# Rolling a matrix in DRAM: row pieces dealt to the DMA engines in blocks of 32 rows instead of 64

## The chip, the cores and the metric

The kernel runs on one core of a Trainium2 chip. The metric is the device time of one execution in microseconds, lower being better.

## The reference

`x` is a matrix of 8192 by 8192 float32 numbers, and `shift` is 100. Each row is rotated to the right by 100 places:

```python
def reference(x, shift):
    return np.roll(x, shift, axis=1)
```

So `out[r, 100:] = x[r, :8092]` and `out[r, :100] = x[r, 8092:]`. There is no arithmetic. 268 MB are read and 268 MB are written; a row is 32 KB.

## The kernel before

The output's columns are divided at `a = 128`, the first multiple of 128 columns (512 bytes) at or above the shift; `g = a - s` is 28.

**Columns 128 and up** are the bulk: 8064 columns of each row, 32,256 bytes, copied straight from the input tensor to the output tensor in DRAM, with no stop on the chip. One `dma_start` (line 41) copies 16 row pieces. The rows are grouped by `xm` and `om`, views of the input and the output with the axes `c` (block), `j`, `e` and the columns. The axis `e` has 16 entries, and within one DMA it is the outer one, so that each of the core's 16 DMA engines copies one row piece. Which rows those are is set by `j`: entry `e` of a DMA is row `4e + j` of a block of 64 rows, so neighbouring engines are four rows apart. The four DMAs of a block take turns between two queues, `engines[j % 2]`: SP (the sync engine) has `j` 0 and 2, ACT (the scalar engine) has 1 and 3. In the last four blocks, 256 rows, every DMA is divided at column `mid` into two, so that the last pieces are shorter. In all SP and ACT issue 248 whole and 16 half DMAs each. The framework gives each queue four semaphores in turn: an issue waits until the DMA four places earlier on its queue has landed, so up to eight DMAs are under way.

**Columns 0 to 127** go through the chip, on GpSimd's queue and VectorE, beside the bulk. Rows are taken in 16 groups of 512, four rows to a partition (`Q = 4`). For each group, GpSimd loads a tile `t` (line 70: the end of a row together with the start of the next, which lie next to each other in memory), and two small pieces of a tile `h` (lines 71 and 74); VectorE copies the rest of `h` from `t` (lines 72 and 75). After all loads are issued, GpSimd stores the 16 tiles `h` to the output (line 78). These tiles all have their own buffers. Nothing in the bulk waits for this part, nor the other way round.

The branch `if a > 512` isn't taken with this shift.

Of the kernel before, what the change touches and what calls it, by code (L numbers as in the profile page):

```python
# [1 line left out]

# [4 lines left out]


@with_exitstack
def kernel(  # L10
    ctx: ExitStack,
    tc: tile.TileContext,
    x: bass.AP,
    shift: int,
    out: bass.AP,
):
    nc = tc.nc
    n_rows, n_cols = x.shape
    s = shift % n_cols
    a = -(-s // 128) * 128  # L20
    g = a - s
    P = nc.NUM_PARTITIONS
    engines = [nc.sync, nc.scalar]
    n_chunks = 16
    rows = n_rows // n_chunks

    xm = x.rearrange("(c e j) w -> c j e w", e=16, j=4)
    om = out.rearrange("(c e j) w -> c j e w", e=16, j=4)
    if a < n_cols:
        blocks = n_rows // 64
        mid = (a + n_cols) // 256 * 128
        for c in range(blocks):
            parts = ((a, mid), (mid, n_cols)) if c >= blocks - 4 and a < mid else ((a, n_cols),)
            for j in range(4):
                for lo, hi in parts:  # L40
                    engines[j % 2].dma_start(out=om[c, j, :, lo:hi], in_=xm[c, j, :, lo - s:hi - s])
    if a == 0:
        return


    if a > 512:
        for i in range(n_chunks):
            r = slice(i * rows, (i + 1) * rows)
            nc.gpsimd.dma_start(out=out[r, :s], in_=x[r, n_cols - s:])
            if g > 0:  # L50
                nc.gpsimd.dma_start(out=out[r, s:a], in_=x[r, :g])
        return

    Q = 4
    n_st = n_rows // (P * Q)
    reads = ctx.enter_context(tc.tile_pool(name="reads", bufs=n_st))  # L60
    heads = ctx.enter_context(tc.tile_pool(name="heads", bufs=n_st))
    xt = x.rearrange("(k p q) c -> k p q c", q=Q, p=P)
    ot = out.rearrange("(k p q) c -> k p q c", q=Q, p=P)
    tiles = []
    for k in range(n_st):
        t = reads.tile([P, Q - 1, a], x.dtype)
        h = heads.tile([P, Q, a], x.dtype)
        lead = bass.AP(tensor=x.tensor, offset=(k * P * Q + 1) * n_cols - s,
                       ap=[[Q * n_cols, P], [n_cols, Q - 1], [1, a]])
        nc.gpsimd.dma_start(out=t[:], in_=lead, single_packet=True)  # L70
        nc.gpsimd.dma_start(out=h[:, Q - 1, :s], in_=xt[k, :, Q - 1, n_cols - s:], single_packet=True)  # L71
        nc.vector.tensor_copy(h[:, :Q - 1, :s], t[:, :, :s])  # L72
        if g > 0:
            nc.gpsimd.dma_start(out=h[:, 0, s:], in_=xt[k, :, 0, :g], single_packet=True)  # L74
            nc.vector.tensor_copy(h[:, 1:, s:], t[:, :, s:])  # L75
        tiles.append(h)
    for k, h in enumerate(tiles):
        nc.gpsimd.dma_start(out=ot[k, :, :, :a], in_=h[:], single_packet=True)  # L78


# [1 line left out]
_INS = ['x', 'shift']  # L82
_OUTS = [((8192, 8192), 'float32')]

_NUMBERS = {'shift': 100}


# [26 lines left out]
```

## Time and profile before

| | before |
|---|---|
| median of 3 runs | 829.13 us (828.62 to 831.27) |
| profiled execution, first to last instruction | 818.3 us |
| median over the span | 10.8 us |
| payload moved, and mean rate | 272.71 MB, 333 GB/s |
| memory traffic, read and written | 656 GB/s over the span |
| VectorE busy, GpSimd busy | 7.8 us, 41.1 us |
| packets of SP's queue, ACT's queue, GpSimd's queue | 8448, 8448, 3328 |

The profiled execution's own time isn't listed apart from its span; the runs' median is 10.8 us longer than the span, and that is what lies ahead of the first and behind the last instruction.

How to read the views. The page gives the span in 40 equal slices of 20.5 us; a digit of the row "DMA" is the mean busy share of the 16 DMA engines in tenths (9 is 90% or more), and "GB/s" is the payload that they moved. A byte copied from DRAM to DRAM counts once in the payload and twice in the memory's traffic. Queue q1 and q10 are the hardware queues on which SP and ACT issue, q0 is GpSimd's. In the rows of DMA issues the last figure is the median time in microseconds from issue to landing. In the view of stretches the last three columns are the TensorE clock (of no account here), the DMA engines' busy share and the GB/s moved. In the view of waits the figures are microseconds in all, times, and the longest.

### The profile page before, as it was taken

Reading aid. Unit: us, or ns where it says so; the run is one execution under the profiler, and the core shown is the slowest. Engines: PE = TensorE matmul, PEld = TensorE weight load, DVE = VectorE, ACT = ScalarE, POOL = GpSimd, SP = SyncE. Lnnn points to the kernel's source line nnn. Section 1 sums busy time; section 2 is a strip of 40 time slices with the busy share of each in tenths; the row PEclk is TensorE's granted clock in tenths of the full one; section 3 lists DMA queues with packets and bytes.
Section 4 is the critical chain, followed back from the end, with each engine's and each line's share of the span. In section 5 each row is a group of like instructions: output and inputs, shape, how many; then the busy total and the mean of one; then the engine's idle time right before and its main releaser. Section 6 shows DMA issues by size and latency. Waiting matters only on the chain. (4 is left out here: it accounts for less than half of the span.)

```text
span 818.3 us, 689 instructions
## 1 busy us (share of the span) xinstructions
DVE 7.8 (1%) x32; POOL 41.1 (5%) x68
## 2 busy tenths in 40 slices
DVE  0000000000000000000000000000000000000000
POOL 3011111111010000000000000000000000000000
DMA  9999999999999999999999999999999999999998
GB/s 304 340 344 338 341 334 345 341 346 350 353 352 357 347 332 321 335 328 326 333 330 323 330 331 330 331 326 333 330 328 334 333 330 339 328 333 334 328 318 294
DMA packets 20229, 272.71 MB, mean 333 GB/s; under 512 B 9472, under 2 KB 9728, under 8 KB 11776
## 3 DMA queue, kind: packets, MB, share of 16 engines
q1 hardware_dynamic: 8448, 132.14, 48.2%
q10 hardware_dynamic: 8448, 132.14, 46.1%
q0 software_dynamic: 3328, 8.39, 4.7%
q14 instruction: 5, 0.04, 0.0%
HBM read 268.44 MB, written 268.44 MB: 656 GB/s over the span
## 5 line engine op out<-in xcount | busy, mean ns | idle before, releaser
L78 POOL DMA_DIRECT2D out_dram<-h x16 | 11.4, 712 | 87.2 <-DMA out_dram<-h 51.7
L70 POOL DMA_DIRECT2D t<-in_x_dram x16 | 12.1, 759 | 32.1 <-DMA h<-in_x_dram 31.3
L74 POOL DMA_DIRECT2D h<-in_x_dram x16 | 8.6, 538 | 85.7 <-DMA t<-in_x_dram 85.7
L71 POOL DMA_DIRECT2D h<-in_x_dram x16 | 8.9, 558 | 23.9 <-DMA h<-in_x_dram 23.9
L72 DVE COPY h<-t 128x300 f32<-128x300 f32 x16 | 5.9, 368 | 190.4 <-DMA t<-in_x_dram 190.4
L75 DVE COPY h<-t 128x84 f32<-128x84 f32 x16 | 3.2, 201 | 0.0
L95 POOL MEMSET const-float32-0.0<- 128x1 f32 x1 | 0.1, 99 | 0.2 <-issue 0.2
L95 POOL MEMSET const-bfloat16-1.0<- 128x1 bf16 x1 | 0.1, 101 | 0.0
L95 POOL MEMSET const-uint8-127<- 128x1 uint8 x1 | 0.1, 99 | 0.0
L95 POOL MEMSET const-float32-1.0<- 128x1 f32 x1 | 0.1, 98 | 0.0
## 6 DMA issues: line engine op xcount, KB each, us to landing
out_dram<-in_x_dram ACTq DMA_DIRECT2D x248, 504.0 KB, 12.5
out_dram<-in_x_dram SPq DMA_DIRECT2D x248, 504.0 KB, 12.5
out_dram<-h POOLq DMA_DIRECT2D x16, 256.0 KB, 63.0
t<-in_x_dram POOLq DMA_DIRECT2D x16, 192.0 KB, 32.6
out_dram<-in_x_dram SPq DMA_DIRECT2D x8, 256.0 KB, 5.9
out_dram<-in_x_dram ACTq DMA_DIRECT2D x8, 256.0 KB, 5.8
out_dram<-in_x_dram SPq DMA_DIRECT2D x8, 248.0 KB, 6.1
out_dram<-in_x_dram ACTq DMA_DIRECT2D x8, 248.0 KB, 6.1
```

Of the source, the lines that this page charges most:

```text
L70: nc.gpsimd.dma_start(out=t[:], in_=lead, single_packet=True)
L71: nc.gpsimd.dma_start(out=h[:, Q - 1, :s], in_=xt[k, :, Q - 1, n_cols - s:], single_packet=True)
L72: nc.vector.tensor_copy(h[:, :Q - 1, :s], t[:, :, :s])
L74: nc.gpsimd.dma_start(out=h[:, 0, s:], in_=xt[k, :, 0, :g], single_packet=True)
L75: nc.vector.tensor_copy(h[:, 1:, s:], t[:, :, s:])
L78: nc.gpsimd.dma_start(out=ot[k, :, :, :a], in_=h[:], single_packet=True)
L95: nc = _bacc.Bacc("TRN2", target_bir_lowering=False, num_devices=1)
```

## The change

The views group rows by `j=2` instead of `j=4`: a block has 32 rows and not 64, entry `e` of a DMA is row `2e + j`, and neighbouring engines are two rows apart instead of four. A block has two DMAs, one for SP (`j` 0) and one for ACT (`j` 1). There are 256 blocks instead of 128, and the last eight, again 256 rows, are halved. The number, sizes, queues and order of the DMAs are those of before; which rows a DMA holds, and so which addresses are under way at one time, differs. The rest of the diff is blank lines, which moves line 41 to 36 and line 109 to 99.

```diff
-    xm = x.rearrange("(c e j) w -> c j e w", e=16, j=4)
-    om = out.rearrange("(c e j) w -> c j e w", e=16, j=4)
+    xm = x.rearrange("(c e j) w -> c j e w", e=16, j=2)
+    om = out.rearrange("(c e j) w -> c j e w", e=16, j=2)
     if a < n_cols:
-        blocks = n_rows // 64
+        blocks = n_rows // 32
         mid = (a + n_cols) // 256 * 128
         for c in range(blocks):
-            parts = ((a, mid), (mid, n_cols)) if c >= blocks - 4 and a < mid else ((a, n_cols),)
-            for j in range(4):
+            parts = ((a, mid), (mid, n_cols)) if c >= blocks - 8 and a < mid else ((a, n_cols),)
+            for j in range(2):
                 for lo, hi in parts:
-                    engines[j % 2].dma_start(out=om[c, j, :, lo:hi], in_=xm[c, j, :, lo - s:hi - s])
+                    engines[j].dma_start(out=om[c, j, :, lo:hi], in_=xm[c, j, :, lo - s:hi - s])
```

## The prediction

> **What bounds the kernel now.** I read the page first (busy shares, the 40 slices, the DMA queues), then the waits of the SP queue, then the stretches side by side, then the DMA view of two stretches with different work in them, and last the writers of the output tensor. From the page:
>
> ```profile
> span 818.3 us, 689 instructions
> DVE 7.8 (1%) x32; POOL 41.1 (5%) x68
> DMA  9999999999999999999999999999999999999998
> GB/s 304 340 344 338 341 334 345 341 346 350 353 352 357 347 332 321 335 328 326 333 330 323 330 331 330 331 326 333 330 328 334 333 330 339 328 333 334 328 318 294
> q1 hardware_dynamic: 8448, 132.14, 48.2%
> q10 hardware_dynamic: 8448, 132.14, 46.1%
> q0 software_dynamic: 3328, 8.39, 4.7%
> HBM read 268.44 MB, written 268.44 MB: 656 GB/s over the span
> out_dram<-in_x_dram ACTq DMA_DIRECT2D x248, 504.0 KB, 12.5
> out_dram<-in_x_dram SPq DMA_DIRECT2D x248, 504.0 KB, 12.5
> ```
>
> No compute engine matters: VectorE and GpSimd are busy 1% and 5% of the span, while the 16 DMA engines are busy from the first slice to the last. The two hardware queues, SP's and ACT's, carry 264.3 of the 272.7 MB; these are the row pieces that go straight from the input to the output. The software queue (the first 128 columns) is 8.4 MB. The page's chain of waits is of no use for the end: it closes with GpSimd's last step at about 270 us, after which the row pieces run on alone for two thirds of the span.
>
> Does issuing hold the row pieces up? The waits of SP's queue, and the row of that line in the view of the output tensor:
>
> ```profile
> SPq L41 <- DMA out_dram<-in_x_dram: 671.1, 260, 4.8
> L41 SPq DMA_DIRECT2D out_dram<-in_x_dram x264: 509/510/842, 0.7 to 811.3; - x132
> DMA to landing us min/median/max: 4.1/12.5/16.8
> ```
>
> SP issues 264 DMAs at 510 ns each, 135 us, and stands 671 us in 260 waits for an earlier row DMA to land. All but its first four issues wait, so each queue keeps four DMAs under way, the two together eight, of 16 rows each: 128 rows. Eight times 516 kB in 12.5 us is 330 GB/s, which is the rate of the slices: the pieces land as fast as something behind the queue takes them, and issue is not it.
>
> Whether that something is the DMA engines or the memory is told by two stretches with different work:
>
> ```profile
> 200.00:250.00 50.00, 0.00 (x0) 4.97 (x7) 1.00 1.00 351
> 300.00:400.00 100.00, 0.00 (x0) 0.00 (x0) 1.00 1.00 328
> 600.00:700.00 100.00, 0.00 (x0) 0.00 (x0) 1.00 0.99 332
> 800.00:819.00 19.00, 0.00 (x0) 0.00 (x0) 1.00 0.84 281
> ```
>
> The last two columns are the DMA engines' busy share and the GB/s moved. The engines are full in the first three, yet they move 351 GB/s between 200 and 250 us, where GpSimd's stores run, and about 330 later. The DMA views of 0 to 270 us (first pair) and of 300 to 780 us (second pair) say why:
>
> ```profile
> DMA packets 8355, 92.42 MB, mean 342 GB/s; under 512 B 3575, under 2 KB 3831, under 8 KB 5729
> q0 software_dynamic: 3133, 7.78, 13.8%
> ...
> GB/s 333 319 332 328 333 336 325 331 331 328 325 323 339 312 333 325 328 339 323 333 333 320 336 339 331 331 333 323 337 337 331 331 336 336 328 336 331 325 336 328
> DMA packets 9847, 158.54 MB, mean 330 GB/s; under 512 B 4917, under 2 KB 4917, under 8 KB 4933
> ```
>
> A row piece touches the memory twice (read and write), a byte of the software queue once (its other side is on chip). Early: 2 x (92.42 - 7.78) + 7.78 = 177.1 MB in 270 us, 656 GB/s. Late: 2 x 158.54 = 317.1 MB in 480 us, 661 GB/s. Counted at the memory the two agree within 1%, though the payload differs by 4% and one stretch is full of pieces under 512 B. So the memory side sets the rate, at about 660 GB/s, and time is bytes divided by that.
>
> The Trainium skill, page "HBM Reference", section "Specifications (TRN2)", puts a stack that two cores share at about 716 GB/s. By that figure 536.9 MB could not take less than an estimated 750 us, so the kernel would stand at 92% of the limit; no run here shows 716.
>
> **The change, part by part.** *Count of work: nothing.* Before, 128 blocks of four DMAs, the last four blocks halved into two column parts; after, 256 blocks of two DMAs, the last eight halved. Either way a queue issues 248 whole DMAs and then 16 half ones, in the same sequence of sizes and with the same wait on the DMA four places earlier, and the halved part is the last 256 rows. GpSimd's and VectorE's lists are the same. So issue (135 us, hidden in 671 us of waiting), the depth of eight DMAs and the tail cost the same; if the tail's 281 GB/s moved by one per cent, it would be 0.2 us. GpSimd's 128 columns are not touched and end some 480 us before the row pieces do; were that cover gone, their 8.39 MB would cost about 25 us at 333 GB/s, but no part of the change takes it away.
>
> *What moves: the addresses at one time.* A row is 32 KB. Before, engine e of the 16 copies rows 4e to 4e+3 of a block of 64, alternating between the queues, then jumps 2 MB ahead: neighbours are 128 KB apart, 16 engines in step cover 2 MB, and each engine returns to the same 128 KB modulo 2 MB whatever it lags. After, engine e copies rows 2e and 2e+1 and jumps 1 MB: neighbours are 64 KB apart, engines in step cover 1 MB, and the fixed slot is 64 KB modulo 1 MB. The engines do lag: a queue's DMA takes 2 x 516 kB / 330 GB/s = 3.1 us on the average, but waits reach 4.8 us and landings range from 4.1 to 16.8 us. An engine that falls two packets behind its neighbour is always a whole block, 1 MB, behind after the change; before, half of the time it is still within the same block. Reads and writes do this alike, since input and output rows have the same place in their tensors.
>
> No row of this trace has a second spacing in it, so the cost is bounded from both sides by how far the rate varies under the present one, where the engines' lags change by themselves. The 23 slices of the page from 307 to 777 us, where row pieces run alone, average 330.2. The four slowest (321, 323, 326, 326) average 324, 1.9% less; the four fastest (339, 335, 334, 334) average 335.5, 1.6% more. Some of this is where a slice cuts a packet, so these are bounds and not readings. The finer slices of 300 to 780 us go down to 312, 5.8% more time per byte, and up to 339, 2.7% less. On about 780 us of full-rate copying, slow ends are +15 us and +45 us, fast ends -12 us and -21 us.
>
> I take half of the first slow end, +0.95% of 780 us: 7.4 us. It is nearest to the middle because nothing but the spacing changes; and to the slow side because the present rate sits on a level that two quite different mixes reach alike, as something does that is close to its limit. From there closer rows can lose much, and spread-out ones had little left to lose.
>
> At one place a rule speaks of spacing itself. The Trainium skill, page "DMA: Bandwidth & Descriptors", section "Latency and other measured facts", has copies between HBM tensors losing rate at large power-of-two row pitches: 207 GB/s per direction at 512 KiB, 164 at 2 MiB, 103 at 4 MiB, with the cause inferred only. Both spacings here lie below its smallest; by it the change is worth nothing (829 us), or something if its fall begins earlier than it was looked for. This trace has 330 GB/s per direction at 128 KB, above all of its figures.
>
> **The sum.** Span 818.3 + 7.4 = 825.7 us. The median of the runs, 829.13, is 10.8 us over the profiled span; this lies outside the first and last instruction and stays. Forecast: 829.1 + 7.4 = 836.5 us. About 0.3% (2.5 us) is what a measurement of this kernel can tell from no change: its three runs lie that far apart.
>
> **The rivals.**
>
> *No difference.* The memory's level is a limit of bytes and not of where they lie; the two mixes at 656 and 661 GB/s speak for it, as do the lags, which scatter the rows before and after. Against it: slices of one mix still differ by 5%. Time: 829 us.
>
> *Faster.* The present 128 KB between neighbours makes some engines collide: sixteen rows that agree in all address bits below 128 KB ask the same part of the memory when they run in step. At 64 KB one more bit differs among the sixteen, so half as many agree in all of them. The place is the whole of the row copying; it decides if collisions that need 128 KB alignment cost more than what is lost by crowding into 1 MB. For it: the payload is well under the fastest slices' rate at times, with the engines' share at 0.99 to 1.00, so engines do stand waiting inside packets. Against it: the flat 660. Price: the fast end, 1.6% of 780 us, -12 us, 817 us; at most -21 us, 808 us.
>
> *Much slower.* The crowding holds engines in step, so that the worst mutual position lasts, not passes. Then the rate is that of the slowest fine slice, 312: +45 us, 874 us; halfway to it, 852 us. For it: with two rows per visit in place of four, every engine jumps twice as often, at the same moment when in step. Against it: landings from 4.1 to 16.8 us show engines not in step.
>
> *That the change does not do what it says* is no rival: the first dimension of each DMA is still 16 rows, one to an engine, and only the stride between them differs.
>
> **How the numbers follow.** Slower by a little (832 to 845 us) 0.45; much slower 0.12; no difference 0.17; faster 0.26. The likeliest is the first, so the time is 836.5 us; its own range is 832 to 845 us. To leave out no more than 2 in 10 the range reaches past the fast end of 817 to 815 us and past halfway to the worst slice, to 857 us: what is left out is the extreme of the fast case and the upper half of the much slower one. Faster 0.26, same 0.17, slower 0.45 + 0.12 = 0.57.
>
> **What would show it.** If right: the profile after has the same counts of packets and DMAs, the engines' share stays at 0.99 to 1.00, the slices from 307 to 777 us average about 327 in place of 330.2, the stretch of 0 to 270 us falls in the same proportion, and the median time to landing goes from 12.5 to about 12.6 us. The tail stays at some 280 GB/s. No difference shows as 330 again; faster as 335 with landings near 12.3 us. The step that can fail is the sign: nothing in this trace fixes it, and a mean over 333 between 300 and 780 us makes the forecast wrong. A change in one stage only, or in SP's 510 ns, would say that it is not the spacing at all.

## The result and the profile after

Over 22 runs each, the changed kernel takes 827.17 us (median; 825.03 to 830.82) and the kernel before 829.68 us (826.53 to 831.27). The ratio is 0.9973, 95% interval 0.9963 to 0.9984. So the change is a gain of 0.27%, clear of noise, and just inside the 0.3% that the prediction had called "same". The forecast, 836.5 us, had the sign wrong. The range, 815 to 857 us, holds the time, but only because it was stretched to the end of the rival "faster"; the range of the forecast's own case, 832 to 845 us, doesn't. Here and below a ratio compares the runs within 1.5% of a kernel's fastest with those of before taken beside them, while a single time is the median of all its runs.

These rows of the page after answer to those shown of before:

```profile
span 823.6 us, 689 instructions
DMA  9999999999999999999999999999999999999998
GB/s 300 345 338 345 325 338 340 332 344 359 341 341 345 338 337 323 332 332 321 329 331 331 324 329 331 332 326 329 332 326 329 336 323 337 320 335 337 321 312 302
q1 hardware_dynamic: 8448, 132.14, 47.8%
q10 hardware_dynamic: 8448, 132.14, 46.7%
HBM read 268.44 MB, written 268.44 MB: 652 GB/s over the span
out_dram<-in_x_dram ACTq DMA_DIRECT2D x248, 504.0 KB, 12.6
out_dram<-in_x_dram SPq DMA_DIRECT2D x248, 504.0 KB, 12.6
```

The waits of SP's queue, the row of its line among the writers of the output, two stretches, and the DMA view of 300 to 780 us:

```profile
SPq L36 <- DMA out_dram<-in_x_dram: 678.2, 260, 4.6
L36 SPq DMA_DIRECT2D out_dram<-in_x_dram x264: 509/510/756, 0.7 to 818.1; - x132
300.00:400.00 100.00, 0.00 (x0) 0.00 (x0) 1.00 1.00 328
600.00:700.00 100.00, 0.00 (x0) 0.00 (x0) 1.00 1.00 331
...
DMA packets 9824, 157.97 MB, mean 329 GB/s; under 512 B 4904, under 2 KB 4904, under 8 KB 4929
```

Packets, queues, issue time (510 ns) and the number of waits (260) are those of before. The engines are full. Between 300 and 780 us 157.97 MB were moved where it was 158.54 MB: 0.36% less, though the runs are 0.27% faster. The prediction's own sign for this stretch (327 GB/s if slower, 330 if the same, 335 if faster) reads 329, no difference. That is the first lesson: one profiled execution of each kernel can't show a difference of this size, and these two point the wrong way.

The span of after is 823.6 us in an execution that took 825.38 us, so 1.8 us lie outside the span. In every execution of which both are on record, 68 of before among them, it is 1.7 to 1.8 us. So the profiled execution of before, with its span of 818.3 us, took about 820 us, less than any timed run of that kernel (the fastest took 826.53 us). The 10.8 us that the prediction and the part ahead of it took for time outside the span are for the most part the distance of one quick execution from the median; why it was quick isn't known. From here on the timed ratios decide, and profiles are read only for differences of several per cent.

### The profile page after: what moved, and what is told of

Its sections match the earlier page's. It is cut to its first block, busy times and chain, and to the rows that moved or that the text cites. A ratio compares the mean times of both kernels' runs of the same rounds, so it can differ in the third digit from the quotient of the medians.

```text
span 823.6 us, 689 instructions
## 1 busy us (share of the span) xinstructions
DVE 7.8 (1%) x32; POOL 41.1 (5%) x68
## 3 DMA queue, kind: packets, MB, share of 16 engines
q0 software_dynamic: 3328, 8.39, 4.7%
```

## The experiments

Except where said, only the deal of the bulk's rows differs. The loop is written as a list of DMAs, so that `J` can be any number and the last 16 DMAs, again 256 row pieces, are the halved ones; `J = 2` and `J = 4` give after and before:

```diff
-            for j in range(2):
+        deals = [(c, j) for c in range(n_rows // (16 * J)) for j in range(J)]
+        for n, (c, j) in enumerate(deals):
...
-                    engines[j].dma_start(...)
+                    engines[n % 2].dma_start(...)
```

**Other powers of two: 1, 8, 64 and 512 rows.** `J = 1`:

> Neighbouring engines one row (32 KB) apart, blocks of 16 rows; all else as in the kernel after. Theory A (the memory's level counts bytes, not places): no move, 829 us or within 0.3% of before. Theory B (crowding costs, the forecast's): since two rows apart did not cost, one row apart shows the cost later: slower by 1% or more, 838 us up. Theory C (alignment at 128 KB costs, closer is better): a further step of the same sign and size as that from four rows to two, 824 to 826 us.

`J = 8`:

> Neighbouring engines eight rows (256 KB) apart, blocks of 128 rows. Theory A: 829 us, within 0.3% of before. Theory B: a little faster than before, 824 to 829 us. Theory C: slower than before by the step from two rows to four or more, 832 us up.

`J = 64`:

> Neighbouring engines 64 rows (2 MB) apart, eight blocks of 1024 rows. Theory A: 829 us. Theory B: 829 us or less. Theory C: clearly slower, because sixteen engines agree in six more address bits than at 32 KB; by the Trainium skill, page DMA: Bandwidth & Descriptors, the rate at a row pitch of 2 MiB is 164 in place of 207, which would be an estimated 829 x 207 / 164 = 1046 us.

`J = 512`:

> Each engine copies its own 512 rows one after the other, neighbours 16 MB apart. Theory A: 829 us. Theory B: 829 us or less. Theory C: much slower than at 2 MB, over 1000 us.

Measured: one row 833.42 us, ratio 1.0056 (1.0030 to 1.0082); eight rows 831.16 us, 1.0024 (1.0011 to 1.0037); 64 rows 1366.87 us (six runs, 1281.79 to 1444.80), 1.5478 (1.5436 to 1.5519); 512 rows 2110.99 us (six runs, 1981.24 to 2258.35). The fastest of the last is 2.39 times the median of before beside it (829.39 us). No theory got all four. Theory A holds at eight rows and fails at one, and at 64 rows by far: places matter, and greatly. Theory B, the forecast's, has the direction right at one row, though not its 1%, and is refuted by 64 and 512 rows: wide spacing is not safe. Theory C has the direction right at 8, 64 and 512 rows (at eight the time stays just under its 832 us) and fails at one row. The page of the kernel with 64 rows, its SP waits, and the same view of waits for 512 rows:

```profile
span 1372.4 us, 689 instructions
DMA  9999999999999999999999999999999999999999
GB/s 214 246 256 226 245 228 227 213 211 221 201 195 191 194 193 191 187 190 189 204 189 185 187 183 203 182 181 183 183 194 189 185 182 182 197 189 191 183 189 168
out_dram<-in_x_dram SPq DMA_DIRECT2D x248, 504.0 KB, 21.8
SPq L36 <- DMA out_dram<-in_x_dram: 1220.9, 260, 9.1
...
SPq L36 <- DMA out_dram<-in_x_dram: 1901.7, 260, 14.9
```

This is the execution of 1374.21 us, 199 GB/s in the mean. The busy digits are the same nines as at 333 GB/s. In the trace's packet records a whole row piece, one packet of 32,256 bytes, takes 1.19 us at the least in both kernels, but 2.57 us in the median with 64 rows and 1.42 us in before. An engine counts as busy for all of that time, so the share tells nothing of a loss of 40%; GB/s and the time to landing (21.8 us in place of 12.5) do. By the Trainium skill, page "DMA: Bandwidth & Descriptors", section "Latency and other measured facts", copies lose rate at power-of-two pitches above 512 KiB. The direction agrees; the estimate from its figures, 1046 us at 2 MiB, is well under the fastest run of 64 rows, 1281.79 us.

**Is it distance or agreement of addresses? 60 rows.** Blocks of 960 rows, then the last 512 rows four apart:

```diff
+    J, J2, split = 60, 4, 7680
+    for lo_r, hi_r, jj in ((0, split, J), (split, n_rows, J2)):
```

> Neighbouring engines 60 rows (1.875 MB) apart in eight blocks of 960 rows, the last 512 rows as in before. The distance is nearly that of 64 rows, but 60 rows is an odd multiple of 128 KB, as the four rows of before are. If distance itself costs (pages of memory far apart): near the 1367 us of 64 rows, over 1250 us. If agreement in the address bits below 2 MB costs: back at the level of before, 822 to 840 us.

Measured: 844.07 us, 1.0190 (1.0167 to 1.0213). Of the 55% that 64 rows cost, 1.9% is left at nearly the same distance, a little above the 840 us of the second reading. So most of the loss is not how far apart the engines are; it goes with a spacing that is a large power of two. In its stretches the rate is steady and a little low:

```profile
400.00:500.00 100.00, 0.00 (x0) 0.00 (x0) 1.00 1.00 321
500.00:600.00 100.00, 0.00 (x0) 0.00 (x0) 1.00 1.00 321
600.00:700.00 100.00, 0.00 (x0) 0.00 (x0) 1.00 1.00 323
```

**Is it closeness or an odd spacing that costs at one row? Three rows**, `J, J2, split = 3, 2, 8160`:

> Neighbouring engines three rows (96 KB) apart in blocks of 48 rows, the last 32 rows dealt two apart. If crowding within a block is what made one row 0.56% slower than before, three rows lies between two (0.9973) and four: 826 to 830 us. If it is the odd row (each queue's rows no longer all of one parity, neighbours that differ in the lowest row bit), it lies near one row: 832 to 835 us.

Measured: 834.00 us, 1.0053 (1.0037 to 1.0069). It is like one row, in a block wider than the 32 rows of after, so the width of the block alone is not what orders these times. That it is oddness was this experiment's other reading. Six and 12 rows below show that even spacings can lose more, so oddness isn't needed for a loss; whether it is what one and three rows lose by isn't shown.

**Is it the bulk itself? The bulk alone, four and two rows apart**, without GpSimd's part:

```diff
-    if a == 0:
-        return
+    return
```

> The bulk alone, four rows apart as in before; columns 0 to 127 of the output are left out. If memory traffic at some 660 GB/s is the bound in all stages, 8.39 MB of software traffic in 660 GB/s is 12.7 us less than before: about 816 us. If the small pieces cost more than their bytes, lower, down to 800 us.

> The bulk alone, two rows apart as in after; columns 0 to 127 are left out. If the 0.27% of the change lies in the bulk copying by itself: 2 us under bulk4. If it lies in how the bulk meets GpSimd's small pieces: equal to bulk4 within 1 us.

Measured: 814.64 us (0.9822, 0.9802 to 0.9841) with four rows and 811.92 us (0.9792, 0.9775 to 0.9809) with two. The difference is 2.7 us, the whole effect of the change and of the same sign, though the two intervals overlap a little. So it can lie in the bulk alone and needs no meeting with the small pieces. Leaving those out saves 14.8 us (1.78% of 829): a little more than the 12.7 us of their bytes at 660 GB/s. Their packets held 4.7% of the engines' time in before, 38 us of the span; that so much less was saved says that bytes at the memory set their price, and not the engines' time. Rows of the page of the kernel with four:

```profile
GB/s 305 329 329 317 329 331 318 332 323 320 329 332 336 312 337 326 331 331 328 332 326 329 336 317 326 334 325 329 328 331 327 330 328 326 329 325 328 328 316 290
HBM read 264.24 MB, written 264.24 MB: 652 GB/s over the span
```

Without the small pieces the early slices fall to the level of the late ones. The 334 to 357 GB/s of before's first stage (its second to thirteenth slice) came with the software queue's bytes, which touch the memory once, as the prediction had counted.

**Six rows**, 192 KB, `J, J2, split = 6, 4, 8064`:

> Neighbouring engines six rows (192 KB, an odd multiple of 64 KB) apart in blocks of 96 rows, the last 128 rows four apart. If agreement in address bits sets the small differences too, it equals two rows apart, 0.997 of before: 826 to 828 us. If the width of the block does, it lies between four rows and eight: 829 to 831 us. If anything but a power of two costs, as three rows and 60 may be read: 832 us up.

Measured: 843.47 us, 1.0168 (1.0136 to 1.0199). It is the third outcome: slower than four and eight rows, though it lies between them, and though its spacing agrees in the same low address bits as two rows.

**Two rows apart, the queues on neighbouring blocks:**

```diff
+        deals = [(c + d, j) for c in range(0, blocks, 2) for j in range(2) for d in range(2)]
```

> Two rows apart as in after, but the two queues copy the same j of two neighbouring blocks, so the two packets that an engine has in hand are 1 MB apart and not adjacent rows. If the adjacency of an engine's two rows is what two and four rows have and one row lacks: 0.5% slower than after, 831 to 834 us. If only the spacing of the engines counts: as after, 826 to 828 us.

Measured: 828.43 us, 0.9990 (0.9974 to 1.0006). This lies between after (0.9973) and before and can't be told from before; it is far from 0.5% slower than after. So the lack of adjacent rows in an engine's hand is not what makes one row slow. But neither is it shown that spacing alone gives the gain of after: with the spacing kept and the order changed, no gain clear of noise is left.

**16 rows**, `J = 16`:

> Neighbouring engines 16 rows (512 KB) apart, blocks of 256 rows. Between 8 rows (1.0024) and 64 rows (1.55). If the loss begins where the Trainium skill, page DMA: Bandwidth & Descriptors, sees it, past a pitch of 512 KiB: 831 to 836 us. If it grows with every bit in which the engines agree: 850 us up.

Measured: 886.52 us (four runs, 873.97 to 890.56), 1.0601 (1.0531 to 1.0672). The large loss begins above eight rows, a spacing of 256 KB. The Trainium skill, page "DMA: Bandwidth & Descriptors", same section as above, has 207 GB/s per direction at 512 KiB of row pitch, against 214 that it calls full; for engines 512 KB apart the measurement says 6% slower. Rows of the stretches, from the execution of 890.56 us:

```profile
400.00:500.00 100.00, 0.00 (x0) 0.00 (x0) 1.00 1.00 301
600.00:700.00 100.00, 0.00 (x0) 0.00 (x0) 1.00 0.99 296
700.00:800.00 100.00, 0.00 (x0) 0.00 (x0) 1.00 0.99 296
```

**Writes alone.** The input isn't read; the bulk is written from a tile on the chip, and columns 0 to 127 are left out:

```diff
-                engines[n % 2].dma_start(out=om[c, j, :, lo:hi], in_=xm[c, j, :, lo - s:hi - s])
+                engines[n % 2].dma_start(out=om[c, j, :, lo:hi], in_=w[n % 8::8, lo - s:hi - s])
```

> The bulk alone, four rows apart, written from a tile on the chip: reading the input is left out, and columns 0 to 127 too. If the memory's traffic of reads and writes together is the bound, the same writes run at well over 330 GB/s, up to whatever the DMA engines take: under 700 us. By the Trainium skill, page DMA: Bandwidth & Descriptors, section Specifications, 435 GB/s is that ceiling, an estimated 608 us for 264 MB. If the engines, the eight DMAs under way or the issue were the bound: about 815 us, as bulk4.

One run: 698.78 us, just under 700. The stretches show more than the total:

```profile
0.00:100.00 100.00, 6.88 (x1) 0.20 (x4) 1.00 0.90 235
100.00:200.00 100.00, 0.00 (x0) 0.00 (x0) 1.00 1.00 368
200.00:300.00 100.00, 0.00 (x0) 0.00 (x0) 1.00 1.00 424
300.00:400.00 100.00, 0.00 (x0) 0.00 (x0) 1.00 1.01 428
400.00:500.00 100.00, 0.00 (x0) 0.00 (x0) 1.00 1.01 428
500.00:600.00 100.00, 0.00 (x0) 0.00 (x0) 1.00 1.01 421
```

The same 16 engines, with the same eight DMAs under way, hold 421 to 428 GB/s once the source is on the chip. Reads alone were not run, so it might be asked whether the engines are slower where the source is in DRAM. The packet records answer it: a whole row piece takes 1.19 us at the least in this kernel and in before alike, and 16 engines at that pace would move an estimated 433 GB/s. The median is 1.19 us here and 1.42 us in the copy, where about a quarter of the pieces go at the quick pace. So an engine can copy from DRAM to DRAM as fast as it writes, and what holds the copy at 330 is the waiting inside the packets: the memory side. Why the first 200 us ran at 235 and 368 GB/s is open; nothing moves for the first 9.4 us, in which the tile is filled.

**Spacing or length of visit?** The change does two things: neighbours come closer, and an engine copies two rows in a block and not four. Here the spacing of before is kept with visits of two rows:

```diff
+        deals = [(c + d, h + j) for c in range(0, blocks, 2) for h in (0, 2) for d in range(2) for j in range(2)]
```

> Neighbours four rows apart as in before, but an engine copies two rows of one block, two of the next, then the other two of each: visits of two rows as in after. If the 0.27% of the change comes from the spacing: as before, 828 to 830 us. If it comes from the shorter visit: as after, 826 to 828 us.

Measured: 831.58 us, 1.0026 (1.0012 to 1.0039), slower than both readings. At four rows the short visit brings no gain; in this order it costs. So shorter visits by themselves don't explain the gain of after.

**12 rows**, `J, J2, split = 12, 4, 8064`, and **32 rows**, `J = 32`:

> Neighbours 12 rows (384 KB) apart in blocks of 192 rows, the last 128 rows four apart. If places that wander are what costs (a block that is no power of two of rows, so that engines with different lags come to one another's places): as six and 60 rows, 841 to 846 us. If the loss at six rows came from that one distance, or agreement in bits below 128 KB counts (12 is an odd multiple of four): 828 to 833 us.

> Neighbours 32 rows (1 MB) apart, blocks of 512 rows. If the loss grows with the number of engines that share a place in a fixed stretch of memory (none at 8 rows, 1.06 at 16, 1.55 at 64): between, about 1.2 to 1.4 of before, 990 to 1160 us. If 64 rows has a cause of its own: about 1.06 to 1.12, under 930 us.

Measured: 12 rows 840.08 us, 1.0125 (1.0104 to 1.0145), close to six and 60 rows, just under the 841 us of the first reading and far from the second; 32 rows 1068.00 us, 1.2830 (1.2777 to 1.2882), between 16 and 64 as the first reading said. The slices of 32 rows:

```profile
span 1073.1 us, 689 instructions
GB/s 251 282 257 274 285 260 288 278 269 271 271 293 281 265 260 263 274 259 257 257 255 262 247 244 249 226 254 228 243 221 250 210 250 207 253 225 245 230 236 236
```

**All spacings together**, as ratios to before:

| rows between neighbours | ratio |
|---|---|
| 1, 2, 4, 8 | 1.0056, 0.9973, 1, 1.0024 |
| 3, 6, 12, 60 | 1.0053, 1.0168, 1.0125, 1.0190 |
| 16, 32, 64, 512 | 1.060, 1.283, 1.548, 2.39 |

One picture fits these three rows; it is inferred, since no view shows memory addresses. Suppose that two packets hinder each other when their rows have nearly the same place within a fixed stretch of memory, some 4 MB (128 rows). With 1, 2, 4 or 8 rows each of the 16 engines keeps to places of its own, whatever it lags, since blocks divide the stretch. With 16 rows two engines share a place, with 32 four, with 64 eight, with 512 all of them, and the loss grows in that order. With 3, 6, 12 and 60 rows the blocks don't divide the stretch, engines that lag wander over one another's places, and a small loss comes up, in no order of spacing. The picture has no place for the 0.56% of one row, and only the runs of 12 and 32 rows put it to the test.

## Why the prediction was right and wrong

**The bound: right.** The memory side sets the time, at about 660 GB/s of reads and writes with spacings in the flat part of the table. Writes alone showed that the engines can move 421 to 428 GB/s, and the bulk alone that 8.39 MB less of traffic is worth 14.8 us, where the count at the memory gives 12.7. But 660 GB/s is no fixed limit of bytes: 64 rows move the same bytes at 391 GB/s over the span of their profile.

**No cost in count, issue, depth and tail: right.** The rows after are the same, 264 issues of 510 ns and 260 waits among them; the tail's last slices are 312 and 302 GB/s where they were 318 and 294.

**What moves: the description was right, the conclusion drawn from it was not.** The prediction said that each engine returns to the same 128 KB modulo 2 MB whatever it lags, and to 64 KB modulo 1 MB after. It went on to count a narrower place as crowding: "closer rows can lose much, and spread-out ones had little left to lose". This is the step that failed, in both halves. Going from four rows to two gained 0.27%, though three rows and one lost 0.53% and 0.56%; the spread-out powers of two lost 0.24% at eight rows and 6% to 139% at 16 to 512. By the picture above, which is inferred, places that are half as wide are still places of one engine alone, and the large losses come where engines share a place, which going from four rows to two doesn't bring about.

**The size: mis-sized with its sign.** The term was +0.95% of 780 us, 7.4 us, half of the way to the slow slices. It measured -0.27% of the whole time, about -2.2 us. The bounds from the slices, -1.6% and +1.9%, do hold it, and they hold all powers of two up to eight. What they can't do is give a sign: the argument that a level reached by two mixes leaves more to lose than to gain says how far a bad spacing may go, not that this one is bad.

**The rivals.** "No difference" comes nearest in size: 829 us against 827.17. Its mechanism, that places don't count, is false; they count by a factor of 2.39 at 512 rows, and 2 and 4 happen to lie on the flat part. "Faster" had the sign; its price of -12 us was about five times too large. Its mechanism, collisions of engines that agree in address bits, fits the rows from 16 up. From two rows to four and from four to eight the steps have its sign too, 0.27% and 0.24%. But it predicts one row to be the fastest, and one row is 0.56% slower than before; and six rows, which agree in the same low bits as two, are 1.7% slower. "Much slower" by engines held in step was not seen.

**The sum.** The 10.8 us outside the span were taken over unchanged into a difference, so the mistake in them did no harm.

**What stays open** is the order within 0.9973 to 1.0056: why two rows beat four and eight, and why one and three are slower. One row's loss is not for lack of adjacency (the queues on neighbouring blocks, 0.9990). The gain of two rows is not the shorter visit alone (1.0026), and the order is not that of the width of the block (three rows, 1.0053) nor of agreement in the low address bits (six rows, 1.0168). So the cause of the 0.27% isn't shown. No version that writes the whole output was faster than after.

## What to carry to other kernels

When a kernel is bound by DRAM traffic, which addresses the 16 DMA engines have in hand at one time is a parameter like any other: blocks of 16 to 128 rows of 32 KB, powers of two, were all within 0.6% here, while spacings of 512 KB and more that are powers of two cost 6% to 139% with the busy digits still at nine. Look at GB/s and time to landing, not at the busy share, to see it. And when a change moves nothing but addresses inside a part that runs have shown to be flat, forecast no difference; scatter between slices of one profile gives the size of what is possible, but no sign.

## What was not expected of the hardware

The loss at large powers of two begins between 256 KB (1.0024) and 512 KB (1.060) of spacing, and nearly goes when the spacing is changed from 64 rows to 60 (1.548 to 1.019). With 32 rows the rate sinks during the execution, from 251 to 293 GB/s in the first 14 slices to 207 to 254 in the last 16. And DRAM writes alone, from a tile on the chip, took some 200 us to come up to their full 428 GB/s.
